# Two square roots moved together on ScalarE, one more buffer and a lower rank for the recurrence of a hybrid mixer

## The chip, the cores and the metric

The kernel runs on one core of one Trainium2 chip. The metric is the device time of one execution in microseconds (us); shorter is better. The core has TensorE (PE in the rows, with PEld its weight loads), VectorE (DVE), ScalarE (ACT), GpSimd (POOL) and SyncE (SP), which here only issues DMAs. Each engine works through its own list of instructions in order, so an instruction that waits holds up all that stand behind it on its engine.

## The reference, cut to what matters

Two layers, each applied to 128 context tokens and 1024 latent tokens (1152 columns in the kernel). A layer projects its normed input once, runs three branches (windowed attention A, a bidirectional gated linear recurrence B, differential attention C), gates and projects each branch, merges them, and projects the sum into the residual. The recurrence is what the change touches:

```python
def rglru_coeffs(x, wa, ba, wx, bx, lam):
    ...
    log_a = -LRU_C * r.astype(jnp.float32) * jax.nn.softplus(-lam.astype(jnp.float32))
    a = jnp.exp(log_a)
    b = jnp.sqrt(-jnp.expm1(2.0 * log_a)) * (i * x).astype(jnp.float32)
    return a, b

def rglru_bidir(x, h0, P):
    ...
    for d in range(2):
        a, b = rglru_coeffs(x, P['lru_wa'][d], ...)
        h = linear_scan(a, b, h0[:, d].astype(jnp.float32), reverse=(d == 1))
        y = y + h
```

and the merge that runs beside it: `m[:, :, k] * ((o * silu(g)) @ w_br)` for each branch k, with `m` the sigmoid of 3 x 1024 more columns of the input projection.

## The kernel before, in words

Everything is float32; a matrix product is made of three TensorE passes over a high and a low part of both operands (lines 158, 159 and 160, helper `mm3`). Each layer has a unit phase (both attentions, and the inputs of the recurrence written out to memory), a tail, and the output projection. The change is in the tail.

The tail is 22 calls of `tail_step`: 8 output tiles for branch C (order 0), 8 for branch A (order 1), 6 for branch B (order 2); the last two tiles of B are done by `tail_last`. A step loads 1024 x 128 weights (`wsraw`, split by ScalarE into `wsh` and by GpSimd into `wsl`) and 512 x 128 branch weights (`wbraw`, split into `wb`). Then come three chunks of 384 columns. A chunk is 24 matmuls into one PSUM buffer `ps_s`; a Tanh on ScalarE that empties it into `mg` (line 1005); and, one chunk later, 12 matmuls of the branch into `ps_s` or `ps_o`, which VectorE multiplies by `mg` and adds to `yr` (lines 106 and 97). `ps_s` has four buffers, `ps_o` has one.

The recurrence is a generator. After each chunk `tail_step` takes one piece of it, and two after the middle chunk, so that it runs in the gaps of the tail. It does four channel tiles of 128 channels in turn (`lru`, twelve pieces each). In one channel tile: `lx` is loaded; ScalarE starts the convolution into `lu` (line 846); VectorE finishes it; `lu` is split into `luhl`; 36 matmuls into `ps_t` and twelve Tanh (line 870) give `lr` and `li` of both directions. Then, for each direction d, ScalarE does Exp into `la` (line 882), Tanh (line 883) and two Squares (line 887), VectorE two products (line 106), ScalarE the square root (line 891), GpSimd three products (line 97) and VectorE three scans (line 907). At the end the directions are added and written out. Exp, Tanh and Square on one side and the square root on the other are served by different function tables of ScalarE; where they alternate, the compiled program holds an ACT_TABLE_LOAD between them. After the recurrence come four pieces that load branch B's input for the last steps, and, in layer 0, pieces of `mod_side`, which sum modulation weights on VectorE (`macc`).

The buffers: ring T has two buffers, used by `lx`, `lu`, `la` of d = 0 and `la` of d = 1 in turn, so the next tile's `lx` takes the buffer of `la` of d = 0, and its `lu` that of `la` of d = 1. Tag `tab` has one buffer. It holds the rotary tables in the unit phase, then is free, and later holds `macc` and one `yr` tile.

What sets the order on each engine: the program is ordered before it runs, by a scheduler that plays it through on a timeline model. Among the instructions ready for an engine it takes the one with the lowest rank. The rank is the place of the instruction in the program as written, less the offset of the enclosing `tc.high_priority(offset=...)`. The count goes back to its old value when such a block ends; each tail step is a block of its own with offset 1500, so all steps count from the same number, and what holds a step back is its buffers. A negative offset adds to the rank.

Of the kernel before, what the change touches and what calls it, by code (L numbers as in the profile page):

```python
# [13 lines left out]
AF = mybir.ActivationFunctionType  # L14
# [5 lines left out]
NTOK = 1152  # L20
# [4 lines left out]

HPO = 2000
TPO = 1500

MLAG = 1
LAG2 = (7, 8)  # L30
# [28 lines left out]
def hybrid_dit_kernel(ctx, tc, I, O):  # L59
# [8 lines left out]
    def ps(tag, *shape):  # L68
        return psp.tile([128] + list(shape), F32, tag=tag, name="ps_" + tag, bufs=PSB[tag])
# [4 lines left out]
    def al(tag, name, *shape):  # L74

        return big.tile([128] + list(shape), F32, tag=tag, name=name, bufs=RINGS[tag])
# [11 lines left out]
    V, A, Pq, T = nc.vector, nc.scalar, nc.gpsimd, nc.tensor  # L88

    def dma(out, in_):  # L90
        nc.sync.dma_start(out=out, in_=in_)
# [4 lines left out]
    def tt(e, out, a, b, op):  # L96
        e.tensor_tensor(out=out, in0=a, in1=b, op=op)  # L97
# [7 lines left out]
    def stt(out, a, s, b, op0, op1):  # L105
        V.scalar_tensor_tensor(out=out, in0=a, scalar=s, in1=b, op0=op0, op1=op1)  # L106
# [29 lines left out]
    def split(hi, lo, raw, eh="A", el="P"):  # L136

        if eh == "A":
            acopy(r(hi), raw)
        else:  # L140
            V.tensor_copy(r(hi), raw)
        tt(Pq if el == "P" else V, r(lo), raw, hi, ALU.subtract)

    def ws_load(wcols, kt):

        raw = al("W", "wsraw", kt, 128)
        wcols(raw)
        hi, lo = al("W", "wsh", kt, 128), al("W", "wsl", kt, 128)
        split(hi, lo, raw)
        return hi, lo  # L150

    def w_in_cols(l, c0):
        def f(lo):
            dma(lo, I["w_in"][l, :, c0:c0 + 128].rearrange("(k p) n -> p k n", p=128))
        return f

    def mm3(out, lh, ll, rh, rl, first, last):
        T.matmul(out=out, lhsT=r(lh), rhs=r(rh), start=first, stop=False)  # L158
        T.matmul(out=out, lhsT=r(lh), rhs=r(rl), start=False, stop=False)  # L159
        T.matmul(out=out, lhsT=r(ll), rhs=r(rh), start=False, stop=last)  # L160
# [665 lines left out]
    def lru(L, ct):  # L826

        l, D = L.l, L.D
        cols, fin = D.cols, D.fin
        PIECES = ((0, 128), (128, 640), (640, NTOK))  # L830
        x = al("T", "lx", NTOK)
        dma(x, xsp[ct])

        wr = al("W", "gwraw", 4, 128)
        w = al("W", "gw", 2, 4, 128)
        wh, wl = w[:, 0], w[:, 1]
        Pq.memset(wr, 0.0)
        for k, nm in enumerate(("lru_wa", "lru_wx")):
            for b in range(2):
                s = slice(64 * b, 64 * b + 64)  # L840
                dma(wr[s, 2 * k:2 * k + 2, s], I[nm][l, :, 2 * ct + b, :, :].rearrange("d c e -> c d e"))
        split(wh, wl, wr)
        yield
        cw = lambda j: cols[:, R_CW + 4 * j + ct:R_CW + 4 * j + ct + 1]
        u = al("T", "lu", NTOK)
        A.activation(out=u, in_=x, func=AF.Identity, scale=cw(2), bias=cols[:, R_CB + ct:R_CB + ct + 1])
        uhl = {}

        def parts(c):
            uhl[c] = al("D", "luhl", 2, 384)  # L850
            split(uhl[c][:, 0, :], uhl[c][:, 1, :], u[:, 384 * c:384 * c + 384])
        for a0, a1 in PIECES:
            e0, e1 = (0, 128) if a0 == 0 else (128, NTOK)
            for j in (0, 1, 3):
                t0, t1 = max(a0, e0 + 2 - j), min(a1, e1 + 2 - j)
                stt(u[:, t0:t1], x[:, t0 + j - 2:t1 + j - 2], cw(j), u[:, t0:t1], ALU.mult, ALU.add)
            if a0:
                parts(0 if a0 == 128 else 1)
                yield
        yield  # L860
        ra = [al("P", "lr", NTOK) for _ in range(2)]
        ri = [al("P", "li", NTOK) for _ in range(2)]
        for c in range(3):
            s = slice(384 * c, 384 * c + 384)
            for d in range(2):
                for k, (dst, hb) in enumerate(((ra, D.hba), (ri, D.hbx))):
                    p = ps("t", 384)
                    m = 2 * k + d
                    mm3(p, wh[:, m, :], wl[:, m, :], uhl[c][:, 0, :], uhl[c][:, 1, :], True, True)
                    A.activation(out=dst[d][:, s], in_=p, func=AF.Tanh, scale=0.5,  # L870
                                 bias=hb[:, 4 * d + ct:4 * d + ct + 1])
            if c == 0:
                parts(2)
            yield
            for d in range(2):
                stt(ri[d][:, s], ri[d][:, s], 1.0, u[:, s], ALU.add, ALU.mult)
        av = []
        for d in range(2):
            kc, nk = D.kcol[:, 4 * d + ct:4 * d + ct + 1], D.nkcol[:, 4 * d + ct:4 * d + ct + 1]
            a = al("T", "la", NTOK)  # L880
            av.append(a)
            A.activation(out=a, in_=ra[d], func=AF.Exp, scale=nk, bias=nk)
            A.activation(out=ra[d], in_=ra[d], func=AF.Tanh, scale=kc, bias=kc)
            for c in range(2):
                s = slice(576 * c, 576 * c + 576)
                t = al("D", "lt2", 576)
                A.activation(out=t, in_=a[:, s], func=AF.Square)
                stt(ra[d][:, s], t, 1.0, ra[d][:, s], ALU.add, ALU.mult)
            yield
        for d in range(2):  # L890
            A.activation(out=ra[d], in_=ra[d], func=AF.Sqrt, scale=0.25)
        yield
        for d in range(2):
            a = av[d]
            st = cols[:, R_ST + 4 * d + ct:R_ST + 4 * d + ct + 1]
            for a0, a1 in PIECES if d == 0 else PIECES[:1] + PIECES[:0:-1]:
                s = slice(a0, a1)
                tt(Pq, ri[d][:, s], ra[d][:, s], ri[d][:, s], ALU.mult)
                if a0 == 0:
                    ini = 0.0  # L900
                elif a0 == 128 and d == 0 or a1 == NTOK and d == 1:
                    ini = st
                else:
                    ini = ra[d][:, a0 - 1:a0] if d == 0 else ra[d][:, a1:a1 + 1]
                if d:
                    s = slice(a1 - 1, a0 - 1 if a0 else None, -1)
                V.tensor_tensor_scan(out=ra[d][:, s], data0=a[:, s], data1=ri[d][:, s], initial=ini,  # L907
                                     op0=ALU.mult, op1=ALU.add)
            e = 127 if d == 0 else 0
            V.tensor_copy(fin[:, 4 * d + ct:4 * d + ct + 1], ra[d][:, e:e + 1])  # L910
            yield
        res = ra[0]
        for c in range(3):
            s = slice(384 * c, 384 * c + 384)
            g = al("D", "lg", 384)
            dma(g, gsp[ct][:, s])
            tt(Pq, res[:, s], res[:, s], ra[1][:, s], ALU.add)
            stt(res[:, s], res[:, s], 0.5, g, ALU.mult, ALU.mult)
        dma(osp[1][ct], res)
# [104 lines left out]
    def y_tile(L, order, j):  # L1024

        L.yr[j] = al("tab" if (order, j) == (2, 7) else "Q", "yr", NTOK)
        if order:
            dma(L.yr[j], ysp[j])

    def wbr_load(L, br, j):  # L1030
        raw = al("W", "wbraw", 4, 128)
        wbr_cols(L.l, br, j)(raw)
        wb = al("W", "wb", 2, 4, 128)
        split(wb[:, 0], wb[:, 1], raw)
        return wb
# [3 lines left out]
    def tail_step(L, n, br, order, j, lag):  # L1039

        mw = ws_load(w_in_cols(L.l, CMG + 1024 * br + 128 * j), KT)
        wb = wbr_load(L, br, j)
        y_tile(L, order, j)
        for c in range(3):
            m = al(MTAG[min(max(n, 7), 9)][c], "mg", 384)
            tail_merge(L, br, j, c, mw, m)

            def branch(c=c, m=m):
                tail_branch(L, order, j, c, L.o[br], wb, m)
            L.late.append(branch)  # L1050
            if len(L.late) > lag:
                L.late.pop(0)()
            next(L.rec, None)
            if c == 1 and not L.recd:
                next(L.rec, None)

    def y_split(L, j, c):
        if c == 0:
# [119 lines left out]
    for l in range(DEPTH):  # L1178
        L = Lay()
# [9 lines left out]
    L = Ls[0]  # L1189
# [46 lines left out]
    for l in range(DEPTH):  # L1236
        L = Ls[l]
# [15 lines left out]
        for n, (br, order, j) in enumerate(steps):  # L1253
            with tc.high_priority(offset=TPO):
                if n == 0:
# [5 lines left out]
                tail_step(L, n, br, order, j, NLAG if n in LAG2 else MLAG)  # L1261
        with tc.high_priority(offset=TPO):
            for _ in L.rec:
# [51 lines left out]
```

## Time and profile before

| what | value |
|---|---|
| median of 3 runs | 2838.39 us (2835.95 to 2838.65) |
| the profiled execution | 2841.75 us; its span from first to last instruction 2840.0 us |
| TensorE busy in the span | 2731.5 us (96%), mean granted clock 0.984 |
| VectorE, ScalarE, GpSimd busy | 1792.6 us (63%), 1285.3 us (45%), 923.9 us (33%) |
| recurrence in the tail, layer 0 and layer 1 | about 845 to 1080 us and 2245 to 2485 us of the span |

Times within the span are counted from its first instruction. A row of a timeline gives the start, the duration, the engine, the line, the operation with its output and inputs, and in brackets how long the engine had stood idle and what released it. A granted clock of 1.00 is the upper of TensorE's two levels, 2.4 GHz.

### The profile page before, as it was taken

What the parts mean: (1) busy time and instruction counts of PE and PEld (TensorE: products, weight loads), DVE (VectorE), ACT (ScalarE), POOL (GpSimd) and SP (SyncE); (2) the same over time, 40 slices, a digit from 0 to 9 for tenths busy, and PEclk for the clock granted to TensorE, in tenths of its full rate; (3) what the DMA queues carried; (4) which work ended last, traced back from release to release, by engine and by line L of the source; (5) the groups of instructions that cost most, each with busy time, mean ns of one, the idle gap of its engine ahead of it and who ended that gap; (6) DMA issues with size and microseconds to landing.
All of it is one profiled execution on the core that took longest, in us unless ns stands there. A gap on an engine that the chain in (4) does not pass through costs nothing.

```text
span 2840.0 us, 44370 instructions
## 1 busy us (share of the span) xinstructions
PE 2731.5 (96%) x16745; PEld 2640.8 (93%) x16745; DVE 1792.6 (63%) x4412; ACT 1285.3 (45%) x2577; POOL 923.9 (33%) x756
## 2 busy tenths in 40 slices
PE   8999999999999999999999999999999998999999
PEld 4889999999999999999989899999999998999999
DVE  5897878775634675824858887887766257612262
ACT  4464554566635651122244555555666266512200
POOL 1333344541223552122204343445312245512230
PEclk9999999999999999999999999999999999999999
DMA  6010011111222344623531010111122223423232
GB/s 231 26 33 29 24 33 34 35 55 51 89 92 75 112 158 152 199 70 114 173 104 34 24 34 20 33 49 32 49 71 71 90 92 101 163 87 106 76 110 83
DMA packets 240852, 228.52 MB, mean 80 GB/s; under 512 B 22706, under 2 KB 218620, under 8 KB 240636
## 3 DMA queue, kind: packets, MB, share of 16 engines
q1 hardware_dynamic: 240636, 225.67, 24.7%
q8 instruction: 132, 2.16, 0.3%
q14 instruction: 84, 0.69, 0.1%
HBM read 172.40 MB, written 53.22 MB: 79 GB/s over the span
## 4 chain that ended last, share of the span: by engine, by line
PE 73%; DVE 13%; ACT 4%; issue 4%; POOL 2%; DMA 2%; SPq 1%; DVEq 0%; ACTq 0%; POOLq 0%
PE ps_s L158 17%; PE ps_s L159 17%; PE ps_s L160 17%; PE ps_o L159 2%; PE ps_o L158 2%; PE ps_o L160 2%; PE ps_o L684 2%; PE ps_t L675 2%; DVE P L515 2%; PE ps_s L513 2%; PE ps_t L542 2%; PE ps_s L514 1%; DVE lr L907 1%; PE ps_s L635 1%; DVE P L106 1%
## 5 line engine op out<-in xcount | busy, mean ns | idle before, releaser
L158 PE MATMUL ps_s<-h,wsh 128*128 128x384 f32 x1440 | 489.5, 343 | 10.3 <-ACT mg L1005 5.6
L160 PE MATMUL ps_s<-h,wsl 128*128 128x384 f32 x1440 | 485.8, 341 | 1.0 <-POOL wsl L97 1.0
L159 PE MATMUL ps_s<-h,wsh 128*128 128x384 f32 x1440 | 485.8, 340 | 0.0
L97 POOL TENSOR_TENSOR wsl<-wsraw,wsh 128x1024 fp32r<-128x1024 f32 x80 | 199.8, 2497 | 357.5 <-ACT wsh L94 167.1
L158 PEld LDWEIGHTS ps_s<-h,wsh 128*128 128x128 f32 x1440 | 272.0, 189 | 13.6 <-ACT mg L1005 6.6
L160 PEld LDWEIGHTS ps_s<-h,wsl 128*128 128x128 f32 x1440 | 271.3, 189 | 1.9 <-POOL wsl L97 1.6
L159 PEld LDWEIGHTS ps_s<-h,wsh 128*128 128x128 f32 x1440 | 272.1, 189 | 0.3
L97 POOL TENSOR_TENSOR qkraw<-qkraw,tab 128x384 f32<-128x384 f32 (+2 forms) x92 | 132.0, 1446 | 338.7 <-DVE qkraw L97 216.6
L515 DVE TENSOR_SCALAR_CACHE_REDUCE P<-ps_s 128x384 f32<-128x384 f32 (+1 forms) x400 | 205.8, 540 | 38.7 <-PE ps_s L514 37.7
L97 DVE TENSOR_TENSOR PT<-ps_t,PT 128x512 fp32r<-128x512 f32 (+2 forms) x304 | 187.8, 626 | 61.6 <-ACT PT L94 60.0
L158 PE MATMUL ps_s<-uwh,h 128*128 128x384 f32 x648 | 222.7, 345 | 2.9 <-ACT h L94 1.9
L159 PE MATMUL ps_s<-uwl,h 128*128 128x384 f32 x648 | 220.6, 342 | 0.0
L160 PE MATMUL ps_s<-uwh,h 128*128 128x384 f32 x648 | 218.5, 345 | 0.0
L94 ACT ACTIVATE PT<-ps_t 128x512 fp32r<-128x512 f32 (+2 forms) x304 | 159.7, 546 | 127.3 <-PE ps_o L160 69.4
L525 ACT ACTIVATE P<-P,csm 128x1152 f32<-128x1152 f32 (+1 forms) x144 | 165.9, 1155 | 96.0 <-DVE csm L101 96.0
L158 PE MATMUL ps_s<-yh,wsh 128*128 128x384 f32 x480 | 164.0, 347 | 14.9 <-ACT mg L1005 10.2
L1005 ACT ACTIVATE mg<-ps_s 128x384 f32<-128x384 f32 x144 | 69.2, 486 | 239.4 <-DVE ps_s L106 122.6
L158 PE MATMUL ps_s<-woh,yh 128*128 128x256 f32 x576 | 164.0, 286 | 0.0
L160 PE MATMUL ps_s<-yh,wsl 128*128 128x384 f32 x480 | 163.0, 342 | 1.0 <-POOL wsl L97 1.0
L160 PE MATMUL ps_s<-woh,yl 128*128 128x256 f32 x576 | 163.8, 285 | 0.0
L159 PE MATMUL ps_s<-wol,yh 128*128 128x256 f32 x576 | 163.6, 284 | 0.0
L159 PE MATMUL ps_s<-yl,wsh 128*128 128x384 f32 x480 | 162.1, 341 | 0.0
(276 smaller groups left out, 7374.5 us busy)
## 6 DMA issues: line engine op xcount, KB each, us to landing
wsraw<-in_w_in_dram SPq DMA_DIRECT2D x80, 512.0 KB, 4.3
ysp<-yr SPq DMA_DIRECT2D x32, 576.0 KB, 5.6
yr<-ysp SPq DMA_DIRECT2D x32, 576.0 KB, 5.4
wuraw<-in_w_in_dram SPq DMA_DIRECT2D x72, 192.0 KB, 3.9
ol<-osp SPq DMA_DIRECT2D x24, 576.0 KB, 4.9
modw<-in_mod_w_dram SPq DMA_DIRECT2D x20, 576.0 KB, 6.1
modw<-in_mod_w_dram SPq DMA_DIRECT2D x16, 512.0 KB, 5.5
woraw<-in_w_out_dram SPq DMA_DIRECT2D x16, 512.0 KB, 3.4
```

Of the source, the lines that this page charges most:

```text
L94: A.activation(out=out, in_=in_, func=AF.Copy, scale=scale)
L97: e.tensor_tensor(out=out, in0=a, in1=b, op=op)
L158: T.matmul(out=out, lhsT=r(lh), rhs=r(rh), start=first, stop=False)
L159: T.matmul(out=out, lhsT=r(lh), rhs=r(rl), start=False, stop=False)
L160: T.matmul(out=out, lhsT=r(ll), rhs=r(rh), start=False, stop=last)
L513: T.matmul(out=p, lhsT=qh, rhs=kk, start=True, stop=False)
L515: V.tensor_scalar(out=S[:, n * c:n * c + n], in0=p, scalar1=1.0, scalar2=NEG, op0=ALU.mult, op1=ALU.max, accum_out=mx[:, mp, c:c + 1])
L525: A.activation(out=Ss[mp][:, 0:n], in_=Ss[mp][:, 0:n], func=AF.Exp, scale=0.125, bias=nm[:, mp:mp + 1], accum_out=acc)
L542: T.transpose(p[:, b, j * 128:(j + 1) * 128], Pm[:, (b0 + b) * 128:(b0 + b + 1) * 128], ident)
L675: T.transpose(p[:, b, 128 * j:128 * j + 128], Ps[2 * t + j][:, (b0 + b) * 128:(b0 + b + 1) * 128], ident)
L684: T.matmul(out=po[:, t, :, :], lhsT=r(vs[kb]), rhs=r(x[:, b, :]), start=kb + k == 0, stop=k == 1 and kb == len(vs) - 1)
L1005: A.activation(out=m, in_=p, func=AF.Tanh, scale=0.5)
```

## The change

Three edits. `la` of direction 1 is taken from `tab` instead of from ring T. The two square roots of a channel tile are put behind the last Square of direction 1 in ScalarE's list; nothing is done to keep other instructions out from between them. The pieces of the recurrence that `tail_step` takes get 90 added to their rank; those outside it (four ahead of the first step, and whatever is left after the last) keep theirs.

```diff
+SPO = -90
...
-            a = al("T", "la", NTOK)
+            a = al(("T", "tab")[d], "la", NTOK)
...
-                A.activation(out=t, in_=a[:, s], func=AF.Square)
+                th = A.activation(out=t, in_=a[:, s], func=AF.Square)
                 stt(ra[d][:, s], t, 1.0, ra[d][:, s], ALU.add, ALU.mult)
             yield
-        for d in range(2):
-            A.activation(out=ra[d], in_=ra[d], func=AF.Sqrt, scale=0.25)
+        with tc.issue_after(th.ins):
+            for d in range(2):
+                A.activation(out=ra[d], in_=ra[d], func=AF.Sqrt, scale=0.25)
         yield
...
-            next(L.rec, None)
-            if c == 1 and not L.recd:
+            with tc.high_priority(offset=SPO):
                 next(L.rec, None)
+                if c == 1 and not L.recd:
+                    next(L.rec, None)
```

## Rows read from the trace of the kernel before

**Rows 1.** Stretches: length; PE, PEld, DVE, ACT, POOL busy (instructions); PE clock; DMA, GB/s.

```profile
845.00:1080.00 235.00, 218.63 (x1199) 214.60 (x1198) 147.53 (x163) 132.34 (x179) 110.74 (x79) 0.97 0.36 117
2245.00:2485.00 240.00, 226.59 (x1251) 222.84 (x1250) 139.86 (x152) 134.66 (x182) 112.29 (x79) 0.98 0.35 113
```

**Rows 2.** Timeline of TensorE: the matmuls that end its long idle times.

```profile
937.97 0.69 PE L158 MATMUL ps_s<-h,wsh 128*128 128x384 f32 x1 [2.61 <-ACT wsh L94]
...
1007.93 0.69 PE L158 MATMUL ps_s<-h,wsh 128*128 128x384 f32 x1 [4.52 <-ACT mg L1005]
...
1078.79 0.69 PE L158 MATMUL ps_o<-oh,wb 128*128 128x384 f32 x1 [5.09 <-DVE yr L97]
...
2344.39 0.69 PE L158 MATMUL ps_s<-yh,wsh 128*128 128x384 f32 x1 [3.81 <-ACT wsh L94]
...
2414.33 0.69 PE L158 MATMUL ps_s<-yh,wsh 128*128 128x384 f32 x1 [4.52 <-ACT mg L1005]
```

**Rows 3.** Busy time in slices of 10 us, columns as in rows 1.

```profile
880.00:890.00 10.00, 10.00 (x59) 10.00 (x58) 6.39 (x7) 6.05 (x8) 5.47 (x4) 1.00 0.16 48
...
930.00:940.00 10.00, 7.39 (x37) 7.07 (x36) 8.04 (x9) 9.94 (x13) 6.34 (x5) 0.90 0.48 159
940.00:950.00 10.00, 10.00 (x54) 10.00 (x54) 8.55 (x8) 4.44 (x6) 6.06 (x6) 0.93 0.65 209
...
1000.00:1010.00 10.00, 5.44 (x25) 4.51 (x24) 8.76 (x7) 4.17 (x4) 7.68 (x7) 0.81 0.19 52
1010.00:1020.00 10.00, 9.38 (x46) 9.07 (x45) 10.00 (x12) 3.52 (x5) 4.86 (x3) 0.85 0.73 264
```

**Rows 4.** Timeline of ScalarE ahead of the idle times at 938 and 1008 us.

```profile
931.85 1.28 ACT L891 ACT_TABLE_LOAD   x1
933.15 1.17 ACT L891 ACTIVATE lr<-lr 128x1152 f32<-128x1152 f32 x1
934.33 1.28 ACT L882 ACT_TABLE_LOAD   x1
935.63 1.35 ACT L882 ACTIVATE la<-lr,nkcol 128x1152 f32<-128x1152 f32 x1
936.88 1.04 ACT L94 ACTIVATE wsh<-wsraw 128x1024 fp32r<-128x1024 f32 x1
...
1004.73 1.35 ACT L846 ACTIVATE lu<-lx,cols 128x1152 f32<-128x1152 f32 x1 [6.48 <-DVE lr L907]
...
1007.39 0.49 ACT L1005 ACTIVATE mg<-ps_s 128x384 f32<-128x384 f32 x1
```

**Rows 5.** Timeline of VectorE ahead of the idle time at 1079 us.

```profile
1071.69 3.99 DVE L106 SCALAR_TENSOR_TENSOR lr<-lr,lg 128x384 f32<-128x384 f32 x2 [0.91 <-POOL lr L97]
1075.61 1.14 DVE L106 SCALAR_TENSOR_TENSOR macc<-modw,sc,macc 128x384 f32<-128x384 f32 x2
1076.67 0.55 DVE L106 SCALAR_TENSOR_TENSOR ps_o<-mg,ps_o 128x384 f32<-128x384 f32 x1
```

**Rows 6.** ScalarE's table loads by line, whole span (count, busy us, mean ns, idle before).

```profile
L891 ACT ACT_TABLE_LOAD x16 | 20.5, 1283 | 0.3
...
L1005 ACT ACT_TABLE_LOAD x12 | 15.4, 1283 | 0.2
...
L882 ACT ACT_TABLE_LOAD x4 | 5.1, 1283 | 0.1
```

**Rows 7.** Timeline of SyncE: the fourth tile written out, branch B's first weights fetched.

```profile
1075.72 0.34 SPq L91 DMA_DIRECT2D osp<-lr  x1
...
1155.71 0.38 SPq L91 DMA_DIRECT2D wbraw<-in_w_br_b_dram  x1
```

**Rows 8.** Timeline of GpSimd: one direction's three products.

```profile
879.99 3.07 POOL L97 TENSOR_TENSOR li<-lr,li 128x128 f32<-128x128 f32 x3 [7.17 <-ACT lr L891]
```

**Rows 9.** Timeline of VectorE: that direction's last two scans.

```profile
882.08 2.06 DVE L907 TENSOR_TENSOR_SCAN lr<-la,cols,li 128x512 f32<-128x512 f32 x1
884.24 1.28 DVE L907 TENSOR_TENSOR_SCAN lr<-la,lr,li 128x512 f32<-128x512 f32 x1
```

## The prediction

> **What bounds the kernel now.** I read the stages first, then TensorE's timeline, then that of whichever engine ended each wait. TensorE sets the pace: through most of the tail a slice of 10 us is full, at 58 to 59 matmuls [rows 3]. Inside the two stretches of the recurrence it isn't. In 235 us it has 1199 matmuls busy for 218.63 us, and in 240 us 1251 for 226.59 us [rows 1]. At the 0.169 us of a full slice (10 us / 59) those matmuls need 203 and 211 us, so the two stretches lose 32 and 29 us, some 61 us in all: about half in idle time (16.4 and 13.4 us), half in matmuls that run longer. No change to the recurrence can win more there. ScalarE is busy for 56% of both stretches [rows 1], so it is not the bound by its sum; what matters is what stands ahead of what in its list.
>
> The reader should see three kinds of wait [rows 2]. **At 1008 us** (and again at 2414 us in layer 1) TensorE waits 4.52 us for `mg`. ScalarE shows why [rows 4]: `lu` of the next channel tile stood in front of it and held the engine idle for 6.48 us, waiting for the scans of direction 1, since `lu` takes the buffer of that direction's `la`. A table load then stood between `lu` and `mg`. **At 938 us** (2344 us in layer 1) it waits 2.61 and 3.81 us for `wsh`, which stood behind the first square root, the load back, and Exp of direction 1: a chain of 5.0 us from 931.85 to 936.88 [rows 4]. **At 1079 us**, in layer 0 alone, it waits 5.09 us for `yr`, which stood behind 3.99 us of the recurrence's last products and a `macc` pair of 1.14 us on VectorE [rows 5].
>
> What a wait costs is more than its idle time, because the matmuls just after it run at a lower granted clock [rows 3]. The slices 1000 to 1020 us have 71 matmuls where 118 would fit: 47 x 0.169 = 8.0 us lost, in slices granted 0.81 and 0.85; a shorter wait lies in them too. The slices 930 to 950 us lose 118 - 91 = 27 matmuls, 4.6 us for 2.61 us of idling. So the surcharge is 2.0 us there. I price the wait at 1008 us at 7.2 us, between 4.52 + 2.0 and 8.0; that at 938 us at 4.6, its twin at 3.81 + 2.0 = 5.8; that at 1079 us at 5.09 + 2.0 = 7.1.
>
> **`la` of direction 1 in `tab`.** The operation is the same, the buffer is there already, and in the tail it is free until `macc` wants it, so the edit costs no instruction. It does two things. Exp of direction 1 no longer waits until the last reader of `lu` is done, so it can run before the first square root. And ring T turns differently: the next `lx` takes the buffer of `lu`, which is free before the square roots, and the next `lu` that of `la` of direction 0, free after that direction's scans. The load of `lx` stands on SyncE's queue before weight loads, so an earlier buffer can only help them. On ScalarE `lu` now waits for the first three scans, not for all six. A direction's scans are 1.5, 2.06 and 1.28 us or more [rows 9], about 5 us, so up to 5 of the 6.48 us of waiting go. Then `mg` starts about 5 us earlier and the 4.52 us vanish: 2 x 7.2 = 14.4 us over both layers. From below, if `lu` is simply put earlier in the list and waits as long, 0; from above, 2 x 8.0 = 16.0. I take 14.4, because the rank edit works the same way at this place. Against it: `macc` in layer 0 can't start until the last scan of the fourth tile, so it may start two directions' scans, some 10 us, later. It is work that goes on beside the remaining steps, so I cost it at nothing; without that cover it would be 10 us.
>
> **The square roots together.** In 16 pairs of a channel tile and direction there are 16 loads for the square root and 16 back, at 1283 ns each [rows 6]: 41.1 us of ScalarE over both layers. If the two roots of a tile stay adjacent, half go, 20.5 us. If a Tanh comes between them, none of that tile's do. A `mg` comes about every 6.1 us (36 matmuls x 0.169), a root takes 1.17 us, so about 1 tile in 5 should be split; I count 6 or 7 adjacent pairs of 8, some 16 us of ScalarE saved. Off the path this is worth nothing by itself. What it is worth on the path is the chain at 938 us: load, root, load, Exp ahead of `wsh`. Exp of direction 1 leaves it, but the second root enters, so the block is 1.28 + 2 x 1.17 + 1.28 = 4.9 us against 5.0 before: the same length, once a tile in place of twice. Whether `wsh` or `mg` stands behind it is luck. I take half of 4.6 + 5.8, that is 5.2 us, with 0 and 10.4 as the ends. Direction 0 starts its products and scans later, by one Exp, Tanh and pair of Squares (1.35 + 1.34 + 1.25 = 3.9 us). Nobody waits for it: the fourth tile is written out at 1075.72 us, and branch B's first weights are fetched at 1155.71 us [rows 7], so 80 us cover a delay of a few us.
>
> The Trainium skill ("ScalarE: Activation LUTs", What ACT_TABLE_LOAD costs) prices a switch at 1283 ns and a drain of 1380 ns, 2.66 us in all. The load agrees to the nanosecond; the drain does not show, for the root starts 0.02 us after its load ends [rows 4]. By the page the 16 loads would be 42.6 us of ScalarE, by the rows 20.5; on the path the sum stays what it is.
>
> **The lower rank.** A chunk is about 38 instructions as written (24 and 12 matmuls, the Tanh, the products), so 90 is somewhat over two chunks: a ready `wsh`, `mg` or `yr` now goes ahead of any piece of the recurrence, and `yr` ahead of `macc`. It adds no instruction. It bears on the wait at 1079 us, where I take half of 7.1, 3.6 us (ends 0 and 7.1), since the 3.99 us of products there were slow on the chip and not placed wrongly. The DMAs of a piece (`gwraw`, `lx`, `lg`, `modw`) move back on SyncE's queue by the same rule and then clear the way for `wsraw`. The recurrence may end two chunks later, 12 us; the same 80 us cover it.
>
> **What is late next.** The order of four engines is dealt anew, by a model that can't know the chip's delays, and a new order makes new waits. By the rows a layer now has three or four long ones. I charge one new wait of the size of the one at 938 us in each layer, 2 x 4.6 = 9.2 us, with none and two in a layer (18.4) as the ends.
>
> **Sum.** 14.4 + 5.2 + 3.6 - 9.2 = 14.0 us won. The profiled execution took 2841.75 us, so it would take 2827.75; the median of the runs shown stands 3.36 us below it, so I predict 2824.4 us, 0.5% faster. With all ends good the gain is 16.0 + 10.4 + 7.1 = 33.5 us, 2804.9; with all ends bad it is a loss of 18.4, 2856.8.
>
> **The rivals.**
> *The waits only move.* ScalarE has slack, the loads that go were off the path, and a newly dealt order has as many waits as the old. For it: 16.4 us idle in layer 0 come from two engines' lists, and the edits bear most on one. Against it: the wait at 1008 us has a cause that the change removes. Gain 14.4 - 9.2 - 4.6 = 0.6 us; time 2837.8.
> *Slower: the scans bunch up on VectorE.* With the roots adjacent, six products on GpSimd and six scans follow at once: two directions x (1.5 + 2.06 + 2.06) = 11.2 us of VectorE, where stretches of ScalarE work lay between the two directions before. A `yr` behind them gives `ps_o` back late, and `ps_o` has one buffer. For it: the wait at 1079 us is just this, at 5.09 us idle. A scan takes 1.28 us with GpSimd at rest, and 2.06 us beside its products [rows 8, 9], so the first direction's scans slow down beside the second's products. Against it: `yr` now ranks ahead of the scans. At 7.1 us each, and without my other new waits, it decides from four of the eight tiles on: 4 x 7.1 = 28.4 against 14.4 + 5.2 + 3.6 = 23.2, so 5.2 us lost, 2843.6; at six tiles 2857.8.
> The Trainium skill ("SBUF — State Buffer", Who interferes with whom) says that a VectorE instruction with two SBUF inputs contends with a GpSimd instruction that reads SBUF, and speaks against bunching; the pair of scans agrees. By it eight tiles would lose at most 8 x 2 x 0.78 = 12.5 us of VectorE, still off the path unless a `yr` stands behind.
> *The roots don't stay together.* A Tanh between them in most tiles leaves 32 loads; the gain of 5.2 goes, the buffer and the rank remain. Time 2829.6, still faster.
>
> **How the numbers follow.** Faster as forecast, with the wait at 1008 us gone: 0.50, about 2812 to 2832. Faster, with split roots: 0.08. More than the sum's good ends allow, since shorter waits go too: 0.05. The waits only move: 0.18. Bunched scans: 0.19, of which a quarter ends within the bound. A measurement here tells 0.2% (5.7 us) from no change. So: faster 0.62, same 0.20, slower 0.18. The range is 2804 to 2847: from the sum with all ends good to the bunching rival at between four and five tiles; it leaves out most of the 0.05 and about half of what is slower.
>
> **What the changed profile would show.** ScalarE: 16 to 20 loads around line 891 and its neighbours in place of 32, and in most tiles the two roots 1.2 us apart. `lu` of a later tile no longer waits 6.48 us for a scan, and no wait of 4.5 us for `mg` follows it. `lx` is issued before the roots. `macc` starts after the last scan. TensorE's losses in the two stretches fall from 61 to about 47 us. I am wrong if `lu` still holds up `mg`, if the block of two roots stands ahead of `wsh` in several tiles, or if `ps_o` waits for `yr` after the scans.

## The result, and the profile after

The changed kernel takes 2931.89 us (median of 4 runs, 2931.24 to 2937.35) where the kernel before took 2838.52 us beside it (4 runs, 2835.95 to 2844.31). The ratio is 1.0324, with a 95% interval of 1.0301 to 1.0348: 3.2% slower, where 0.5% faster was forecast. In the changed kernel the lines stand two further down (158 becomes 160, 94 becomes 96, 106 becomes 108, 846 becomes 848), and three from the square roots on (891 becomes 894, 907 becomes 910, 943 becomes 946, 1005 becomes 1008).

The page of the changed kernel, busy time of the engines, and TensorE with its granted clock in 40 slices of 73 us:

```profile
PE 2744.9 (94%) x16745; PEld 2654.4 (91%) x16745; DVE 1756.3 (60%) x4412; ACT 1274.5 (43%) x2569; POOL 933.4 (32%) x756
...
PE   8999999999999589996999999999999995999999
...
PEclk9999999999999899997999999999999997899999
```

The span grew by 90.4 us, from 2840.0 to 2930.4. TensorE's busy time grew by 13.4 us of that (2731.5 to 2744.9), so the other 77.0 us are idle time. Four slices stand out: the 14th and 15th, the 19th, and the 34th. The 14th, 15th and 34th lie in the two recurrences; the 19th lies behind the recurrence of layer 0.

TensorE's waits in the changed kernel (total, times, longest):

```profile
PE ps_t L160 <- ACT luhl L96: 60.9, 4, 24.6
PE ps_t L946 <- DVE macc L108: 17.7, 3, 9.1
PE ps_s L160 <- ACT mg L1008: 10.5, 3, 4.7
PE ps_o L160 <- DVE yr L99: 10.3, 4, 4.8
```

The same view of the kernel before:

```profile
PE ps_s L158 <- ACT mg L1005: 15.8, 11, 4.5
PE ps_o L158 <- DVE yr L97: 13.4, 4, 5.1
...
PE ps_t L943 <- DVE macc L106: 5.7, 3, 2.2
...
PE ps_t L158 <- ACT luhl L94: 4.3, 4, 1.5
```

The waits for `mg` and `yr`, at which the prediction looked, shrank from 29.2 to 20.8 us. The wait for `luhl`, the recurrence's own input on TensorE, grew from 4.3 to 60.9 us, and that for `macc` from 5.7 to 17.7. These four together make 60.2 of the 77.0 us; the rest is spread over small waits. The long ones by themselves, on TensorE's timeline:

```profile
975.60 1.33 PE L160 MATMUL ps_t<-luhl,gw 128*128 128x384 f32 x3 [6.13 <-ACT luhl L96]
...
1005.37 0.33 PE L162 MATMUL ps_s<-h,wsl 128*128 128x384 f32 x1
1030.29 1.33 PE L160 MATMUL ps_t<-luhl,gw 128*128 128x384 f32 x3 [24.59 <-ACT luhl L96]
...
1362.36 2.73 PE L946 MATMUL ps_t<-one,macc 128*128 128x1 f32 x12 [9.10 <-DVE macc L108]
1373.32 0.56 PE L946 MATMUL ps_t<-one,macc 128*128 128x1 f32 x2 [8.23 <-DVE macc L108]
...
2489.61 1.33 PE L160 MATMUL ps_t<-luhl,gw 128*128 128x384 f32 x3 [23.88 <-ACT luhl L96]
```

At 1005 us the tail has nothing more for TensorE, and the next in its list is a matmul of the third channel tile that has no input yet. It stands still for 24.59 us, and for 23.88 us at the same place in layer 1. Three stretches of the changed kernel (length; PE, PEld, DVE, ACT, POOL busy; granted clock; DMA):

```profile
1000.00:1100.00 100.00, 71.57 (x377) 69.07 (x376) 60.17 (x76) 53.76 (x71) 44.38 (x31) 0.84 0.30 97
1300.00:1400.00 100.00, 77.55 (x462) 76.93 (x461) 75.16 (x135) 14.26 (x26) 23.85 (x11) 0.85 0.50 157
2400.00:2500.00 100.00, 64.60 (x308) 61.90 (x307) 55.22 (x63) 50.23 (x68) 49.52 (x34) 0.78 0.32 102
```

In the kernel before, whose work lies 70 to 90 us earlier, the same times hold 477, 684 and 515 matmuls at 0.93, 0.98 and 0.97.

**Why `luhl` is late.** Read backwards from 1030 us. ScalarE and then VectorE of the changed kernel, up to the split that TensorE waits for:

```profile
1010.20 1.28 ACT L894 ACT_TABLE_LOAD   x1
1011.49 2.21 ACT L894 ACTIVATE lr<-lr 128x1152 f32<-128x1152 f32 x2
1018.25 1.35 ACT L848 ACTIVATE lu<-lx,cols 128x1152 f32<-128x1152 f32 x1 [4.54 <-DVE lr L910]
1029.71 0.52 ACT L96 ACTIVATE luhl<-lu 128x384 fp32r<-128x384 f32 x1 [10.12 <-DVE lu L108]
```

```profile
1019.66 2.03 DVE L910 TENSOR_TENSOR_SCAN lr<-la,cols,li 128x512 f32<-128x512 f32 x1
1021.61 2.65 DVE L108 SCALAR_TENSOR_TENSOR lu<-lx,cols,lu 128x126 f32<-128x126 f32 x4
1024.18 1.27 DVE L910 TENSOR_TENSOR_SCAN lr<-la,lr,li 128x512 f32<-128x512 f32 x1
...
1026.48 3.14 DVE L108 SCALAR_TENSOR_TENSOR lu<-lx,cols,lu 128x512 f32<-128x512 f32 x3
```

The two roots of the second tile stand together, as meant, and `lu` does wait for three scans instead of six (4.54 us, 6.48 us in [rows 4]). But all of this now lies in a hole of the tail. The kernel before does the same work some 70 us earlier. The tiles leave for memory (`osp`) at these times:

| tile of layer 0 | before | after |
|---|---|---|
| first | 907.76 | 977.41 |
| second | 960.95 | 1032.12 |
| third | 1016.75 | 1078.62 |
| fourth | 1075.72 | 1208.26 |

The 70 us are lost in the first tile. Its twelve Tanh run from 853.91 to 889.41 us before and from 868.38 to 946.99 us after, a few at a time:

```profile
869.30 0.58 ACT L872 ACTIVATE lr<-ps_t,hba 128x384 f32<-128x384 f32 x1
888.33 0.58 ACT L872 ACTIVATE li<-ps_t,hbx 128x384 f32<-128x384 f32 x1 [1.88 <-PE ps_t L162]
909.14 0.56 ACT L872 ACTIVATE lr<-ps_t,hba 128x384 f32<-128x384 f32 x1
...
928.61 0.58 ACT L872 ACTIVATE li<-ps_t,hbx 128x384 f32<-128x384 f32 x1 [4.22 <-PE ps_t L162]
...
946.99 0.58 ACT L872 ACTIVATE li<-ps_t,hbx 128x384 f32<-128x384 f32 x1
```

The gaps are 16 to 21 us, about the length of a tail step (three chunks of 6.1 us and the waits): TensorE takes matmuls of the recurrence only where a step has run dry. That is a reading of these gaps; the run that leaves the matmuls their rank, below, bears it out. The rank counts from the same number in every step, because the count goes back when a step's block ends, and a step writes about 126 instructions. So 90 more puts a piece behind nearly everything of any step that has its buffers, not behind two chunks.

**Who needs the recurrence early.** SyncE's queue of the changed kernel around the hole, and of the kernel before at the same work:

```profile
1032.12 0.32 SPq L93 DMA_DIRECT2D osp<-lr  x1
1034.89 0.80 SPq L93 DMA_DIRECT2D ol<-osp  x2
```

```profile
960.95 0.32 SPq L91 DMA_DIRECT2D osp<-lr  x1
961.32 0.42 SPq L91 DMA_DIRECT2D ol<-osp  x1
```

Directly behind the second tile's write-out stands the load of branch A's first input (`ol`, split into `oh`). Its two buffers are of ring P (seven buffers), the ring in which `lr` and `li` of the channel tiles live. By the order in which the program asks for these buffers, they come free only at the end of the second tile; no view names the buffers, so this is read from the code. The ninth to the sixteenth step multiply that input by their branch weights. Before, it was fetched at 961 us, 36 us ahead of its first use, in the kernel before:

```profile
997.42 0.34 PE L158 MATMUL ps_s<-oh,wb 128*128 128x384 f32 x1
```

After, the tail ran out of work at 1005 us and the load was issued at 1035 us (one of the two in its row). The 24.59 us of idle time end with a matmul of the recurrence, but the tail itself stands still for longer. Its first matmul after 1005.37 us waits for `oh`:

```profile
1042.90 0.44 PE L160 MATMUL ps_s<-oh,wb 128*128 128x384 f32 x1 [0.68 <-ACT oh L96]
```

So what the tail lacked was branch A's input. In layer 1 it stands still from 2465.40 to 2501.81 us and goes on with the same matmul.

The second, smaller loss is in layer 0 alone: the sums (`macc`) start late behind the fourth tile, which leaves at 1208.26 us, pile up on VectorE, and hold the matmuls at 1362 and 1373 us. What causes it isn't shown: in the run with 30 in place of 90 the fourth tile leaves as late as 1156.80 us without a long wait for `macc`, and in the run whose matmuls keep their rank it leaves at 1090.81 us, with a wait of 8.90 us.

### The profile page after: what moved, and what is told of

It is laid out like the page before. It is cut to its first block, busy times and chain, and to the rows that moved or that the text cites. A ratio compares the mean times of both kernels' runs of the same rounds, so it can differ in the third digit from the quotient of the medians.

```text
span 2930.4 us, 44387 instructions
## 1 busy us (share of the span) xinstructions
PE 2744.9 (94%) x16745; PEld 2654.4 (91%) x16745; DVE 1756.3 (60%) x4412; ACT 1274.5 (43%) x2569; POOL 933.4 (32%) x756
## 4 chain that ended last, share of the span: by engine, by line
PE 71%; DVE 14%; ACT 5%; DMA 5%; issue 3%; POOL 1%; SPq 1%; ACTq 0%; DVEq 0%; POOLq 0%
PE ps_s L160 17%; PE ps_s L161 17%; PE ps_s L162 17%; PE ps_o L161 2%; PE ps_o L160 2%; PE ps_o L162 2%; DVE lr L910 2%; PE ps_o L686 2%; PE ps_t L677 2%; PE ps_s L515 1%; DVE P L517 1%; PE ps_t L544 1%; PE ps_s L516 1%; DVE macc L108 1%; DMA wsraw<-in_w_in_dram 1%
```

## The experiments

Each ratio is against runs of the kernel before on the same chip, with its 95% interval. "Block" is the `with tc.high_priority` around the pieces. In the expectations, theory A is the one above (the rank makes the recurrence late, and branch A's input with it); C is about where the wait goes that the buffer removes; D says that the block by itself, at any offset, changes the ranks. Other letters are rivals and say there what they hold.

### Each edit alone

**The rank back to 0, everything else of the change kept.**

```diff
-SPO = -90
+SPO = 0
```

> The changed kernel with the added rank back at 0; the buffer and the paired roots stay. Theory A (the rank starves the recurrence: each tail step counts its rank from the same number, so 90 more puts a piece behind whole later steps, TensorE takes its matmuls only where a step has run dry, and the recurrence comes a tile too late for the loads that step 8 needs): the loss goes, 2815 to 2840 us, the four channel tiles are written out at about 908, 961, 1017 and 1076 us as before, and no wait of TensorE for luhl is over 2 us. Theory B (the paired roots and the turned ring bunch the scans and hold up lu): the loss stays in good part, above 2880 us, with waits for luhl of 10 us and more.

Measured: 1.0090 (1.0073 to 1.0107), 2866.89 us. The first two tiles leave at 942.44 and 995.13 us, and the waits for `luhl` fall to 12.2 us. Neither theory's range holds this. Going back to 0 brings back some 65 us, most of the loss, but not all. All root pairs are split (32 loads), and there is a new wait, TensorE and then VectorE ahead of it:

```profile
988.52 0.69 PE L160 MATMUL ps_s<-oh,wb 128*128 128x384 f32 x1 [8.95 <-DVE yr L108]
```

```profile
979.48 2.04 DVE L910 TENSOR_TENSOR_SCAN lr<-la,cols,li 128x512 f32<-128x512 f32 x1
981.43 4.73 DVE L108 SCALAR_TENSOR_TENSOR lu<-lx,cols,lu 128x126 f32<-128x126 f32 x4
986.09 1.27 DVE L910 TENSOR_TENSOR_SCAN lr<-la,lr,li 128x512 f32<-128x512 f32 x1
...
987.92 0.54 DVE L108 SCALAR_TENSOR_TENSOR yr<-mg,ps_s 128x384 f32<-128x384 f32 x1
```

Most of this wait needs neither the buffer nor the roots: the run of the block alone, below, has one of 6.76 us for `yr` at 983.77 us.

**The rank alone.**

```diff
+SPO = -90
...
-            next(L.rec, None)
-            if c == 1 and not L.recd:
+            with tc.high_priority(offset=SPO):
                 next(L.rec, None)
+                if c == 1 and not L.recd:
+                    next(L.rec, None)
```

> The kernel before with the rank edit alone. Theory A: nearly the whole loss, 2900 to 2950 us; the twelve Tanh of the first channel tile spread over some 80 us where they took 20, and a wait of 20 us or more for luhl in each layer. Theory B: within 15 us of before, 2825 to 2853 us.

Measured: 1.0219 (1.0201 to 1.0236), 2903.45 us. The hole is there without the buffer and the roots, at the same place and of about the same length:

```profile
1024.68 1.33 PE L160 MATMUL ps_t<-luhl,gw 128*128 128x384 f32 x3 [25.74 <-ACT luhl L96]
```

**The buffer alone.**

```diff
-            a = al("T", "la", NTOK)
+            a = al(("T", "tab")[d], "la", NTOK)
```

> The kernel before with la of direction 1 in the extra buffer, and nothing else. Theory A, and the prediction's term for this edit: faster by up to 14 us, 2822 to 2840, with the 6.5 us wait of lu for the scans shortened and the 4.5 us wait for mg gone. Theory B: slower by 10 us or more, since macc and the turned ring come late.

Measured: 1.0102 (1.0085 to 1.0118), 2867.7 us. The edit that was to win 14.4 us costs 1%. That is the size that theory B named, but not by way of `macc`, whose waits are 7.1 us here and 5.7 before. ScalarE and TensorE of this kernel show both halves of it:

```profile
1007.15 1.35 ACT L846 ACTIVATE lu<-lx,cols 128x1152 f32<-128x1152 f32 x1 [0.66 <-DVE lr L907]
...
1025.32 0.52 ACT L94 ACTIVATE luhl<-lu 128x384 fp32r<-128x384 f32 x1 [5.87 <-issue]
```

```profile
1025.90 1.33 PE L158 MATMUL ps_t<-luhl,gw 128*128 128x384 f32 x3 [5.47 <-ACT luhl L94]
```

`lu` waits 0.66 us in place of 6.48, and the 4.52 us wait for `mg` is gone. But the next tile's `luhl` takes a buffer of ring D (three buffers), where `lg` of the tile before still stands, until VectorE has done its last products (`lr<-lr,lg`, 3.94 us, up to 1025.2 us). The wait moved from ScalarE to TensorE.

**The roots alone.**

```diff
-                A.activation(out=t, in_=a[:, s], func=AF.Square)
+                th = A.activation(out=t, in_=a[:, s], func=AF.Square)
...
-        for d in range(2):
-            A.activation(out=ra[d], in_=ra[d], func=AF.Sqrt, scale=0.25)
+        with tc.issue_after(th.ins):
+            for d in range(2):
+                A.activation(out=ra[d], in_=ra[d], func=AF.Sqrt, scale=0.25)
```

> The kernel before with the two roots put behind the last Square, and nothing else; la of direction 1 still waits for the buffer of lu. Theory A: within 12 us of before, 2828 to 2850, with 16 to 20 table loads in place of 32. Theory B (bunched scans): slower by 10 us or more, with TensorE waiting for yr behind scans.

Measured: 1.0044 (1.0029 to 1.0060), 2852.03 us. The table loads fall from 32 to 20, 15.4 us of ScalarE, and the kernel is slower. TensorE waits 5.50 us for `yr` at 1029.71 us, which on VectorE stands behind the scans of both directions and a product `ol<-ol,oh` of 3.72 us; the same wait comes once in layer 1. The waits for `wsh`, at which the roots were aimed, do shrink, from 7.6 to 1.3 us. They are outweighed: all waits for `yr` grow from 13.6 to 19.3 us, those for `mg` from 15.8 to 20.1.

**Buffer and roots, without any block.**

```diff
-            with tc.high_priority(offset=SPO):
-                next(L.rec, None)
-                if c == 1 and not L.recd:
-                    next(L.rec, None)
+            next(L.rec, None)
+            if c == 1 and not L.recd:
+                next(L.rec, None)
```

> The changed kernel with the pieces called as before, with no block: extra buffer and paired roots alone. Theory D: faster than the run that had the block at rank 0 (2867 us) by 8 to 18 us, 2848 to 2859, with the first tile written out before 925 us. If the block does nothing: 2862 to 2870.

Measured: 1.0030 (1.0018 to 1.0043), 2849.47 us: together less than the buffer alone, and no more than the roots alone. The parts don't add up; each makes a whole new order. Against the run with the block at 0 (2866.89 us) it is 17 us faster, as theory D expected. The longest waits for `luhl` are 5.79 us. The longest wait of all is for `macc`. Its sums start on VectorE at 1087.62 us, directly behind the fourth tile's last scan, which holds `tab` until then:

```profile
1103.82 0.59 PE L946 MATMUL ps_t<-one,macc 128*128 128x1 f32 x2 [9.11 <-DVE macc L108]
```

### What the rank does

**The block at offset 0 on the kernel before.** The same four lines as in the rank alone, with `SPO = 0`.

> The kernel before with the new block around the pieces, at an offset of 0: no rank is added, but the count goes back at the end of each block. Theory D (the block alone delays the recurrence, since the tail's instructions behind a piece now rank as if the piece were not there): the first tile is written out at about 937 us in place of 908, as in the run with only the sums lowered, and the time is 2850 to 2862. If the block does nothing: as before, 2835 to 2846.

Measured: 1.0071 (1.0054 to 1.0087), 2861.59 us. A block that shifts nothing costs 20 us. Without it, the instructions of a piece raise the count for what is written behind them; with it, the count goes back, so what follows gains rank over the pieces. The first two tiles leave at 936.15 and 991.75 us, 30 us later than before.

**30 in place of 90.**

```diff
+SPO = -30
```

> The kernel before with 30 in place of 90 added to the rank. Theory A says that 90 already puts a piece behind every instruction of any tail step (a step is some 126 instructions, and all steps count from the same number), while 30 leaves most pieces inside their own step: the first tile's twelve Tanh take 20 to 40 us, the second tile is written out before 1000 us, no wait for luhl over 10 us, time 2830 to 2865. If the loss grew with the number itself, a third of it would be seen: about 2861, with a wait for luhl of some 8 us.

Measured: 1.0151 (1.0128 to 1.0174), 2884.08 us, with the long wait already at 25.2 us, against what theory A expected of 30. Of the loss, 0.71% is the block's, so a third of the offset brings 0.80 of the 1.48% that 90 adds to the block, and a hole as long: the effect isn't in proportion.

**90 only from the eighth step on, 0 ahead of it.**

```diff
+            with tc.high_priority(offset=SPO if n >= 7 else 0):
```

> The kernel before with 90 added to the rank only from the eighth tail step on; the first two channel tiles keep their rank. Theory A (the second tile must be done before the branch A input of step 8 can be loaded, since both use ring P): the second tile is written out at about 961 us and the waits of 25 us for luhl go, so 45 to 75 us of the rank's 62 us come back or more, 2835 to 2865; what stays is the late last tile and macc, near 1350 us. If the lower rank costs something everywhere (other orders, more waits), most of the loss stays: 2880 and more.

Measured: 1.0071 (1.0047 to 1.0095), 2860.67 us, the block's price and no more. The second tile leaves at 991.92 us and no wait for `luhl` is longer than 1.77 us, though the fourth tile is as late as 1173.67 us and the two waits for `macc` stay (9.30 and 8.58 us). From the eighth step on the offset costs nothing on balance: its two waits for `macc` stand against waits for `mg` of 6.0 us, where the block alone has 30.1. Its own price is paid in the first seven steps.

**90 for everything but the recurrence's matmuls.**

```diff
-                    mm3(p, wh[:, m, :], wl[:, m, :], uhl[c][:, 0, :], uhl[c][:, 1, :], True, True)
+                    with tc.high_priority(offset=-SPO):
+                        mm3(p, wh[:, m, :], wl[:, m, :], uhl[c][:, 0, :], uhl[c][:, 1, :], True, True)
```

> The kernel before with the rank edit on all of a piece but its matmuls, which keep the rank that they had. Theory A (TensorE's order is where the pieces starve): the first tile's twelve Tanh take about 20 us again, the second tile is written out before 1000 us, and at least 40 of the 62 us come back, 2835 to 2865. If ScalarE, VectorE or SyncE are where they starve, the loss stays above 2880.

Measured: 1.0023 (1.0007 to 1.0039), 2849.07 us. With only these matmuls at the old rank, 2.19% becomes 0.23%. The first tile leaves at 917.13, the second at 965.53 us, and the waits for `luhl` are 7.6 us. So what the rank cost, it cost through TensorE's list. The time is even under that of the block alone (2861.59 us). Whether the lower rank of the other instructions helps there, or the second block around the matmuls, after which the count goes back too, no run tells apart.

**90 only for what follows the recurrence (`macc` and branch B's loads).**

```diff
+            with tc.high_priority(offset=SPO if L.recd else 0):
```

> The kernel before with 90 added to the rank of the modulation sums alone (the pieces after the recurrence); the recurrence keeps its rank. The prediction's term for the wait at 1079 us says that a yr ahead of macc wins up to 7 us, in layer 0 alone: 2832 to 2840. Theory A would have it that the sums starve too and are late at the end of the tail (two waits of 8 to 9 us for macc near 1350 us): 2850 to 2865.

Measured: 1.0054 (1.0039 to 1.0068), 2858.72 us. Layer 1, which has no sums, changed as well; that led to the run of the block alone. With that run known, the offset on the sums neither wins nor loses anything clear of noise (1.0054 and 1.0071, with intervals that overlap), and the two long waits for `macc` that theory A expected don't come (3.7 us in all).

**90 in the other direction.**

```diff
+SPO = 90
```

> The kernel before with 90 taken off the rank of the pieces, so that the recurrence goes ahead of the tail. Theory A: the tiles are written out earlier than 908, 961, 1017 and 1076 us, no wait for luhl over 6 us; the price is wsh and mg behind pieces on ScalarE. Time 2825 to 2860. If the tail's instructions are what must go first, slower than 2860.

Measured: 1.0026 (1.0011 to 1.0041), 2848.91 us. The tiles leave 6 to 17 us earlier than before, and TensorE waits more for `mg`: 24.5 us in ten waits, the longest 7.62. Earlier doesn't beat the kernel before either, though it is 13 us faster than the same block at 0.

**90, with a head start of 16 pieces ahead of the first step.**

```diff
-LRU0 = 4
+LRU0 = 16
```

> The kernel before with the rank edit, and 16 pieces of the recurrence ahead of the first step in place of four, one channel tile more. The rank is as low as in the changed kernel. Theory A (TensorE idles because the second tile is late for step 8): the second tile is written out before 975 us, no wait for luhl over 8 us, and at least 35 of the 62 us come back, 2840 to 2868. If the lower rank costs by itself: 2880 and more.

Measured: 1.0260 (1.0241 to 1.0279), 2916.78 us, slower than the rank alone, against what was expected. The first tile left at 878.64 us, but the second had its matmuls starved in the same way and left at 1002.81 us. TensorE and SyncE:

```profile
1045.58 1.33 PE L160 MATMUL ps_t<-luhl,gw 128*128 128x384 f32 x3 [29.67 <-ACT luhl L96]
```

```profile
1042.70 0.32 SPq L93 DMA_DIRECT2D osp<-lr  x1
1043.07 0.42 SPq L93 DMA_DIRECT2D ol<-osp  x1
```

With twelve more pieces done early the load came to stand behind the third tile's write-out. The tail stands still from 1011.46 to 1054.63 us and again goes on with a matmul of `oh`, so this fits a deadline set by ring P, but a tile ahead bought nothing.

### Where the buffer's wait goes

A fourth buffer for ring D would be the plain test; no run has it. `lg` was taken out of ring D instead, into the buffer of `li` of direction 0, which is free by then:

```diff
-            g = al("D", "lg", 384)
+            g = ri[0][:, s]
```

**With the buffer.**

> The kernel before with the extra buffer for la of direction 1, and with the gate pieces lg of a tile loaded into its own li of direction 0 once that direction's scans have read it, in place of ring D. Theory C (the extra buffer frees lx and lu early, but the next tile's luhl still waits in ring D for lg of the tile before, which is used last; so the wait only moves from lu on ScalarE to luhl on TensorE): the wait of 5.5 us for luhl goes, and of the buffer's loss of 27 us at least 12 come back, 2835 to 2855. If the loss has its cause in the order of ScalarE (split table loads, lu ahead of the second root), little changes: 2860 to 2875.

Measured: 1.0035 (1.0024 to 1.0046), 2852.99 us; the buffer alone was 1.0102. The waits for `luhl` fall from 14.1 to 6.5 us, none over 3.2. In their place stands a wait of 6.34 us for `yr` at 1073.25 us.

**On the kernel before, without the buffer.**

> The kernel before with lg in li of direction 0 and nothing else. Theory C: here lu's own buffer comes free no earlier, so lu on ScalarE still waits for the last scan; 2825 to 2845, and no wait for luhl gets longer. Against it: the load of lg now stands in SyncE's queue until direction 0 is scanned, and weights stand behind it: 2845 to 2860.

Measured: 1.0014 (1.0003 to 1.0025), 2846.36 us, so that the move is no gain by itself, and the 4.52 us wait for `mg` stays.

**With the buffer, the roots and the block at 0.**

> The changed kernel with the added rank at 0 and lg in li of direction 0. Theory C: the waits of 5.3 us for luhl go and the time is 8 to 20 us under that of buffer and roots alone (2867), 2840 to 2860; what stays are the waits for yr behind the scans. Otherwise 2860 to 2875.

Measured: 1.0039 (1.0021 to 1.0056), 2853.46 us, against 1.0090 without the move: it gives back half a per cent here too. The waits of 8.9 us for `yr` stay.

**The whole change, with the matmuls and the sums at the old rank and `lg` moved.**

```diff
-                    mm3(p, wh[:, m, :], wl[:, m, :], uhl[c][:, 0, :], uhl[c][:, 1, :], True, True)
+                    with tc.high_priority(offset=-SPO):
+                        mm3(p, wh[:, m, :], wl[:, m, :], uhl[c][:, 0, :], uhl[c][:, 1, :], True, True)
...
-            g = al("D", "lg", 384)
+            g = ri[0][:, s]
...
-            with tc.high_priority(offset=SPO):
+            with tc.high_priority(offset=0 if L.recd else SPO):
```

> The changed kernel with the recurrence's matmuls and the modulation sums at their old rank and lg in li of direction 0; extra buffer, paired roots and the lower rank of the recurrence's other instructions stay. If theories A and C name all that matters: 2835 to 2855, a gain over the changed kernel of 75 us or more. A time under 2835 would beat the kernel before. If the three edits cost something else together: above 2860.

Measured: 1.0112 (1.0090 to 1.0133), 2872.12 us. It brings back 60 us of the change's 92 and isn't the mended kernel that was expected. The long hole is gone (longest wait for `luhl` 8.62 us), but 24.6 us for `luhl`, 18.8 for `ps_o`'s `yr` and 12.6 for `mg` remain. Why they are more here than with each repair alone stays open.

No version beat the kernel before. The nearest were `lg` moved (1.0014), the rank without the matmuls (1.0023) and the raised rank (1.0026).

## Why the prediction was wrong, step by step

**What bounds the kernel** held. TensorE sets the pace, and 77.0 of the 90.4 us are its idle time. The rest fits the surcharge that the prediction had seen in small, matmuls at a lower granted clock after a wait: the mean granted clock fell from 0.984 to 0.968.

**The lower rank is the step that failed.** The prediction put it so: "A chunk is about 38 instructions as written [...] so 90 is somewhat over two chunks", and "The recurrence may end two chunks later, 12 us; the same 80 us cover it." Both halves are wrong.
- The size: ranks of different steps don't follow one another, since the count goes back at the end of a step's block; the kernel's description said so, and the sum didn't use it. The recurrence ends 132.5 us later (1075.72 to 1208.26), not 12, and the first tile alone 70 us; 30 in place of 90, less than a chunk, already costs 1.5% with its block.
- The cover: 80 us is the distance of the fourth tile from branch B's weights [rows 7], the last consumer. The first one is branch A's input, which needs the second tile out of ring P, and had 36 us between its fetch and its first use. No row of the prediction looked there. The price is 2.19% (62 us) for the rank alone, where 3.6 us were to be won. Of that the block alone makes some 20 us, though an offset of 0 reads like no edit. That the tail waits for branch A's input in the hole is in the trace, in the changed kernel and in the three other runs that have the hole (the rank alone, 30 in place of 90, the head start); that ring P holds that input back is read from the queues and the code. That the hole goes when the first seven steps, or the matmuls, keep their rank is shown.

**`la` of direction 1 in `tab`** had the right mechanism for the first wait: the wait for `mg` at 1008 us [rows 2, 4] goes, and `lu` waits 0.66 us in the buffer's own run. "So I cost it at nothing" was said of `macc` alone. There the cover held in the buffer's own run (waits of 7.1 us in all), but not with buffer and roots, where one wait for `macc` is 9.11 us, near the 10 us that the prediction named for want of cover. Ring D, in which the next `luhl` meets the last `lg`, wasn't followed. The term of +14.4 us measured as 27 us lost alone, some 19 of which (1.0102 to 1.0035) went when `lg` left ring D. The rest comes with the new order and has no one cause shown.

**The roots** were right in the count where they stand alone (20 loads, 16 to 20 forecast), and wrong in the whole change, where ScalarE's table loads by line are 24:

```profile
L894 ACT ACT_TABLE_LOAD x12 | 15.4, 1283 | 0.2
L1008 ACT ACT_TABLE_LOAD x9 | 11.5, 1283 | 0.2
L872 ACT ACT_TABLE_LOAD x3 | 3.8, 1283 | 0.1
```

Twelve loads for sixteen roots mean four pairs of eight adjacent, not six or seven; in the third tile a `mg` stands between them at 1057.34 us. The 5.2 us for the chain at 938 us were aimed rightly: in the roots alone the waits for `wsh` shrink by 6.3 us. But the new order's waits for `yr` and `mg` cost more, and the roots alone lose 0.44%, with 15.4 us of ScalarE saved. In the whole change the waits for `wsh` are 7.4 us, as before.

**The charge for new waits**, 9.2 us, was a guess at the size of waits seen before. The new ones are 24.6, 23.9, 9.1, 8.2, 6.4 and 6.1 us.

**The rivals.** The bunched scans were real but not the cause: in the roots alone they hold `yr` for 5.50 us, once in a layer, where the rival counted four to eight tiles. (With the rank back the wait is 8.95 us, but one of 6.76 us comes with the block alone.) In the change itself the second tile's scans lie in the hole. The chances don't quite follow from their parts: the three faster cases add up to 0.63 and three quarters of the bunched one to 0.14, where 0.62 and 0.18 stand. The loss came by a way that no rival named, and the upper end of the range, 2847 us, lay 85 us below the result.

## What to carry to other kernels

Read a rank offset against what it competes with: if the count goes back at the end of each block, an offset of a fraction of a block's instructions can already mean "nearly last", and a block with offset 0 is an edit too. To say that a delay is covered, look for the first consumer of anything that the delayed work holds, its buffers above all, and not only for the reader of its last result. An added buffer moves a wait to the next ring that the same data pass through, so follow them to the engine that sets the pace, and test each edit alone and with the others, because the effects of orders that are dealt anew don't add up.

## What the runs showed of the hardware

After the long hole TensorE comes back at a lower granted clock (its lower level, 1.2 GHz, is 0.50): the 10 us from 1030 us hold 30 matmuls at a granted clock of 0.57, those from 1040 us 48 at 1.00; from 2490 us it is 28 at 0.53. In a full slice of the kernel before there are 58 to 59 [rows 3], so each hole costs more than it shows as idle.

A 512-column scan took 2.03 us beside GpSimd's products (at 1019.66 us) and 1.27 us after them (at 1024.18 us), as in the kernel before [rows 9]. It isn't so for each: the one at 1016.93 us took 1.28 us although GpSimd is listed as busy all through it. A group of four convolution products took 4.73 us with the rank back, at 981.43 us, where GpSimd was busy for 3.8 us of that time, and 2.65 us in the changed kernel at 1021.61 us, where it was busy for 1.01 us. The Trainium skill ("SBUF — State Buffer", Who interferes with whom) says that a VectorE instruction with two SBUF inputs contends with a GpSimd instruction that reads SBUF; the pairs agree with it and the scan at 1016.93 us doesn't, and none of the runs tried it by itself.
